# Spreading the experts' weights: two accumulated 128-column products per token, or one of 256 columns with its halves added on GpSimd

## The chip, the cores and the metric

One core of a Trainium2 chip runs the whole program. The metric is the device time of one execution in microseconds; smaller is better. TensorE multiplies, VectorE (DVE in the profile), ScalarE (ACT) and GpSimd (POOL) work on tiles in SBUF, and all DMAs are issued from SyncE's queue (SP).

## The reference, cut to what matters

Two transformer blocks run one after the other on 256 tokens of 1024 features. The second has two layers; each ends in a product-key mixture over 16384 experts, of which a token takes 16 in each of 8 heads. In the first layer 256 tokens of context take part as well.

```python
def peer_block(hb, w_q, sub_keys, u_tab, v_tab):
    ...
    top_s, pos = lax.top_k(cand_s, PEER_TOPK)
    expert = jnp.take_along_axis(cand_i, pos, axis=-1)      # i1 * 128 + i2
    g = jax.nn.softmax(top_s, axis=-1)
    u = u_tab[expert]
    act = jax.nn.gelu(jnp.einsum('nhkd,nd->nhk', u, hb).astype(jnp.float32))
    w = (g * act).astype(hb.dtype)
    return jnp.einsum('nhk,nhkd->nd', w, v_tab[expert])
```

## The kernel before

The kernel gathers no experts. It computes the hidden value of every expert for every token, multiplies it by a weight that is zero for all but the chosen ones, and sums over all experts. For that each token needs its 128 weights `g` spread over a matrix of 128 first keys by 128 second keys.

Arithmetic near float32 is had by cutting each operand in two float32r parts (`split`, lines 198 and 199: a cast on ACT, a subtraction on DVE) and taking three products (`mac`, lines 232 to 234).

The change touches `spread`. For a block of 128 tokens it takes four tokens per turn of a generator: 32 turns for a block, four blocks in the first layer and two in the second, 192 turns in all. One turn does this:

- DVE builds `E` (line 1053, four instructions of 512 float16 values): a one-hot of the first key, a one-hot of the second key, and the second one multiplied by each of two float16 parts of the weight. The four tokens lie side by side, innermost, so that the columns of one token are 4 values (8 bytes) apart.
- TensorE makes, for each token, two products with the same stationary operand: first key's one-hot by each part of the weighted second key's one-hot. Both are of 128 columns, and the second is added to the first in PSUM (line 1057). Eight matmuls, eight weight loads.
- ACT takes the PSUM bank of four tokens to the tile `st`, where a token's values lie 64 bytes apart (line 1058). After four turns SP sends `st` to the memory `Gd` (line 1060).

`pG` is a bank of the PSUM ring `C`, which has four; `E` lies in the ring `wb` (three slots), `st` in `k8` (seven), and the ring `k2` (six) holds the outputs of line 1100 and small tiles of `choose`.

`ahead` runs this beside the main work: it goes through the 128 tiles of experts, and after each tile (`hidden`: a load, the two parts, 24 products of 256 columns per 256 tokens, a gelu on ACT) lets the generators of `choose` and `spread` take as many turns as the plan (`P0`, `P1`) says. So a stretch of `hidden` products alternates with one or two turns of `spread` on TensorE. The hidden values go to the memory `kept`. After `ahead`, `experts` loads the weights (`b<-G`) and the hidden values (`k<-kept`) again and sums.

The order of the instructions on each engine is that of a scheduler which runs when the program is built; each engine then works through its own list in order.

Of the kernel before, what the change touches and what calls it, by code (L numbers as in the profile page):

```python
# [18 lines left out]
P = 128  # L19
# [7 lines left out]
# columns of the first layer's modulation: on the tensor engine; before the experts  # L27
EARLY = 16
MID = 40
# the context's hidden values taken early: tiles up to here beside the first block, and beside the second's start  # L30
FILL = (27, 39)
# the last tiles of experts are summed bank by bank
TAIL = 4
# steps of the work beside: at the points of the mixers, of the feed-forwards (norm, pieces), of the second block's start
# [3 lines left out]
# when the choices, then the spreadings, of the blocks of tokens start, and at what pace  # L38
P0 = ((5, 0.8), (38, 0.95), (72, 1.15), (124, 1.1), (38, 0.9), (83, 0.8), (121, 0.9), (169, 0.95))
P1 = ((5, 0.75), (41, 1.0), (45, 0.5), (85, 0.85))  # L40
# choices that begin beside the scores, of the two layers
EAR = (1, 1)
# tiles of experts whose hidden values the second layer takes before the sums
# [3 lines left out]
class Side:  # L47
    """Where a stream of work keeps its tiles: weights, PSUM for products and transposes, slots."""
# [5 lines left out]
class Net:  # L54
# [19 lines left out]
    @staticmethod  # L74
    def done(gen):
        """all the steps of a generator; its result"""
        while True:
            try:
                next(gen)
            except StopIteration as e:  # L80
                return e.value

    def pace(self, side, rate):
        """other work that goes on beside: `rate` steps of it at each point where the main work lets it in"""
        self.side, self.rate, self.due = side, rate, 0.0
# [7 lines left out]
    def beside(self, gen, n=1):  # L93
        """all the steps of a generator, with `n` breaths after each; its result"""
        while True:
            try:
                next(gen)
            except StopIteration as e:
                return e.value
            self.breathe(n)  # L100

# [42 lines left out]
    def rsqrt(self, ss, n, m, sfx):  # L144
        """(ss / n + eps) ** -0.5 of the columns ss[:m rows]"""
# [8 lines left out]
    def norm_T(self, sd, xt, scale, bias=None, dst=None, between=None):  # L154
        """rms-normalised rows of xt [128, 2, 1024], transposed to [128, 8, 256], times scale plus bias
        (columns [128, 8], a value per feature), in two parts where the side's products want them"""
# [39 lines left out]
    def split(self, hi, lo, src):  # L196
        """src as the sum of two float32r parts"""
        self.nc.scalar.copy(hi, src)  # L198
        self.nc.vector.tensor_sub(lo, src, hi.bitcast(F32))  # L199

    def cut_in_two(self, shape, raw):
        """the two parts of a block of weights, in the ring of slots of the phase"""
# [10 lines left out]
    def weights(self, sd, src, n=512, order=None):  # L213
        """src [128, k, n], row block by row block: two blocks are loaded at a time and cut in two parts"""
# [11 lines left out]
    def mac(self, out, a, b, first, last):  # L226
        """out += a.T @ b, operands in two parts each"""
# [11 lines left out]
    def tok_steps(self, sd, src, hT, order=(0, 2, 4, 6), also=None, apart=False):  # L239
        """hT.T @ src for both blocks of tokens, and for both of `also`: banks [128 tokens, 512];  # L240
        apart: one block after the other, with all the weights at hand"""
# [18 lines left out]
    @staticmethod  # L260
    def cut(f, a, b):
        """the columns a to b of both parts"""
        return tuple(None if t is None else t[:, a:b] for t in f)

# [1 line left out]
    def mixer(self, l, x):  # L266
# [5 lines left out]
        # queries, keys and values of the attention heads, tokens on the partitions  # L272
# [20 lines left out]
        # columns: kc kc | vc vc | ks kw | vs vw | gates | i | f  # L293
# [17 lines left out]
        # windows of 32 tokens, 16 apart, the odd tokens of a window on the upper partitions  # L311
# [11 lines left out]
        # norms and rotation of the attention heads  # L323
# [25 lines left out]
        # gates of the matrix memory  # L349
# [22 lines left out]
        # q and k of the matrix memory: a feature per partition, convolved along the tokens  # L372
# [17 lines left out]
        # the rest of the matrix memory's inputs  # L390
# [14 lines left out]
        # transposes: pairs of heads, the second of a pair on the upper partitions  # L405
# [26 lines left out]
        # compressed keys and values  # L432
# [67 lines left out]
        # attention: groups of four heads (moba, selected, window), of which a unit takes the even or the odd ones  # L500
# [69 lines left out]
        # matrix memory, all tokens at once  # L570
# [155 lines left out]
    def ada_early(self):  # L726
        """the first columns of the first layer's modulation of both streams, a value per feature and partition:
        [128, 2 streams, 6 * 8]; work comes in steps"""
# [17 lines left out]
    def ada_rest(self, i0, i1):  # L746
        """the rest of the first layer's modulation, then the second's: columns i0 to i1 of the two in a row"""
# [23 lines left out]
    def modulation(self, l, part):  # L771
        """the biases, and (1 + scale) * gain in place of the scales; part 0: before attention, part 1: after"""
# [7 lines left out]
    def gate(self, sd, col, n, g=None):  # L780
        """col [128, 8], a value per feature, as a row of 512 features on every partition"""
# [8 lines left out]
    def qkv(self, sd, l, hT, rope, hT2=None):  # L790
        """the heads' queries and keys, normalised and rotated, features by tokens, and the values;
        a chunk of four heads (two of keys, two of values) at a time.
        hT2: of another 256 tokens the keys and values too, not rotated"""
# [3 lines left out]
        if rope:  # L797
            # gain * cos, and the partner's gain * sin
# [20 lines left out]
    def heads(self, sd, n, pks, gain, turn, dst, v):  # L819
        """a chunk's heads of two blocks of tokens from PSUM: normalised, rotated and transposed to dst; or values to v"""  # L820
# [37 lines left out]
    def attention(self, sd, qT, segs, sink=None, window=False):  # L858
        """softmax over the keys of segs [(kT, v)], 256 keys each; the heads' outputs, features by tokens"""
# [79 lines left out]
    def key_scores(self, l, hs, ss):  # L939
        """the scores of the keys, per block of 128 tokens [128 tokens, (head, half), 128 keys], head by head"""  # L940
# [22 lines left out]
    def choose(self, sd, s):  # L963
        """of a block of 128 tokens [128 (head, choice), 4, 128 tokens], float16: the two key numbers and two parts
        of GSCALE times the weight"""
# [29 lines left out]
        # the place in the list gives the ranks of the two keys  # L995
# [46 lines left out]
    def spread(self, r, Gd, nb):  # L1042
        """the weights of a token's experts, a matrix [128 first keys, 128 second keys] per token;
        four tokens per turn of the generator"""
        nc = self.nc
        for q in range(P // NT):
            st = self.t("k8", [P, P, NT])
            for m in range(0, NT, 4):
                n = q * NT + m
                pG = self.p("C", [P, 4, P])  # L1050
# [4 lines left out]
                for j in range(4):  # L1055
                    for i in range(2):
                        nc.tensor.matmul(pG[:, j], E[:, 0, :, j], E[:, 2 + i, :, j], start=i == 0, stop=i == 1)  # L1057
                nc.scalar.activation(st[:, :, m:m + 4], pG.rearrange("p n e -> p e n"), AF.Copy, scale=1 / GSCALE)
# [4 lines left out]
    def routing(self, l, hs, Gd, order, early, plan):  # L1063
        """the scores of the keys, and the rest of the routing as a plan for `ahead`: of the blocks of tokens in order
        [(block, place in Gd)] the choice, then the spreading of the weights;
        the first `early` choices begin beside the scores. plan: when each choice and each spreading starts, and its pace"""
# [17 lines left out]
    def hidden(self, l, e, hs, aside=False):  # L1084
        """gelu(u . h) of the tile e of experts: [128 experts, 256 tokens for each of hs]"""
# [17 lines left out]
    def ahead(self, l, hs, kept, n, plan, done=0):  # L1103
        """the hidden values of the first n tiles, kept in memory while the weights are still to come;
        the first `done` lack the first 256 tokens only.
        plan: [(start, a generator, its turns per 256 tokens of a tile)]"""
# [17 lines left out]
    def experts(self, l, hs, Gd, kept, side):  # L1124
        """sum over all experts of weight * gelu(u . h) * v; hs: functions giving the parts of h for 256 tokens each.
        side: a generator of other work, a step of which goes with every second tile of experts.
        Yields (block of tokens, half of the features, the sums)"""
# [58 lines left out]
    def context(self):  # L1186
        """the context's side of the first layer, which hangs on nothing before it, up to its experts"""
# [21 lines left out]
    def context_end(self):  # L1209
        """the output of the context's attention, and what its experts work on"""  # L1210
# [14 lines left out]
    def fill(self, e0, e1):  # L1225
        """the context's hidden values of the first layer's tiles e0 to e1"""
# [4 lines left out]
    def block2(self, x):  # L1231
# [4 lines left out]
        # the first layer of the stream itself  # L1236
# [28 lines left out]
        # the second layer  # L1265
# [22 lines left out]
def _rows(w):  # L1288
    """[.., 1024, n] -> [.., 128, 8, n]"""
# [4 lines left out]
def _tiles(w, c=512):  # L1294
    """[.., 1024, n * c] -> [.., n, 128, 8, c]"""
# [7 lines left out]
def _cols(v):  # L1303
    """[.., 1024] -> [.., 128, 8]"""
# [4 lines left out]
def layout(i):  # L1309
# [20 lines left out]
    # second block  # L1330
# [17 lines left out]
    # constants  # L1348
# [58 lines left out]
```

## Time and profile before

| | |
|---|---|
| time, median of 3 runs | 3616.06 us |
| lowest and highest run | 3615.57 and 3619.06 us |
| span of the profiled execution | 3617.9 us |
| TensorE busy | 98% of the span |
| VectorE, ScalarE, GpSimd busy | 66%, 42%, 1% |
| turns of `spread` | 192, between 1287 and 3225 us |

The profiled execution shows a span of 3617.9 us, 1.8 us above the median of the runs and inside their range. Records of TensorE overlap, since matmuls are pipelined: a busy share of 98% is time in which some matmul was on its way, and the pace is read from the spacing of the starts or from counts in a stretch.

### The profile page before, as it was taken

The numbers are of one execution on the slowest core, as the hardware profiler recorded it, in microseconds if no ns is written. First come the engines' busy times: TensorE is split into PE (matmuls) and PEld (weight loads), VectorE is DVE, ScalarE is ACT, GpSimd is POOL, SyncE is SP. The second block draws the span as 40 slices with busy tenths as digits, with TensorE's granted clock in tenths as the row PEclk, the third lists the DMA queues.
The fourth block names the chain that finished last, engine by engine and source line by source line (L and its number), as shares of the span: only waits on it lengthen the run. The fifth ranks groups of instructions, "written<-read, shape, count | busy, mean of one in ns | idle before, by whom it ended". The sixth has DMA issues, their size and how long they took to land.

```text
span 3617.9 us, 58159 instructions
## 1 busy us (share of the span) xinstructions
PE 3548.2 (98%) x22400; PEld 3116.1 (86%) x22400; DVE 2372.8 (66%) x5225; ACT 1528.0 (42%) x2557; POOL 51.9 (1%) x72
## 2 busy tenths in 40 slices
PE   8999989999999999999999999999999999999999
PEld 6677776899899999999998888888878999998777
DVE  6666776655754778767647655554476778767666
ACT  5543455544643433333333322222254545545443
POOL 1000010000000000000000000000000000000000
PEclk9999999999999999999999999999999999999999
DMA  6556644566522754445579877776223777779986
GB/s 222 165 181 200 202 154 131 188 202 201 161 94 83 228 181 164 170 171 177 178 239 290 265 246 243 235 225 188 76 77 113 213 232 233 247 268 297 293 256 192
DMA packets 329383, 712.76 MB, mean 197 GB/s; under 512 B 28305, under 2 KB 170257, under 8 KB 322705
## 3 DMA queue, kind: packets, MB, share of 16 engines
q1 hardware_dynamic: 329104, 709.05, 61.4%
q8 instruction: 175, 2.87, 0.3%
q14 instruction: 104, 0.84, 0.1%
HBM read 606.44 MB, written 102.50 MB: 196 GB/s over the span
## 4 chain that ended last, share of the span: by engine, by line
PE 82%; DMA 8%; DVE 6%; issue 1%; ACT 1%; SPq 0%; POOL 0%; DVEq 0%; POOLq 0%; ACTq 0%
PE psA L232 12%; PE psA L233 12%; PE psA L234 12%; PE psC L233 9%; PE psC L234 9%; PE psC L232 9%; PE psC L1057 5%; DMA wb<-in_v 3%; DMA k<-kept 3%; PE psB L233 3%; PE psB L232 3%; PE psB L234 3%; DVE k L199 2%; PE psB L230 1%; DVE ws L199 1%
## 5 line engine op out<-in xcount | busy, mean ns | idle before, releaser
L198 ACT CAST ws<-w 128x1024 fp32r<-128x1024 f32 (+1 forms) x528 | 548.3, 1038 | 1032.0 <-PE psA L233 738.4
L199 DVE TENSOR_TENSOR ws<-w,ws 128x1024 fp32r<-128x1024 f32 (+1 forms) x528 | 636.7, 1207 | 411.5 <-ACT ws L198 405.9
L232 PE MATMUL psA<-b,ws 128*128 128x256 f32 x2760 | 784.7, 284 | 0.0
L234 PE MATMUL psA<-b,ws 128*128 128x256 f32 x2760 | 773.9, 280 | 0.9 <-DVE ws L199 0.3
L233 PE MATMUL psA<-b,ws 128*128 128x256 f32 x2760 | 773.2, 280 | 0.0
L232 PEld LDWEIGHTS psA<-b,ws 128*128 128x128 f32 x2760 | 521.8, 189 | 0.6 <-ACT k L1100 0.2
L234 PEld LDWEIGHTS psA<-b,ws 128*128 128x128 f32 x2760 | 519.3, 188 | 2.6 <-DVE ws L199 2.5
L233 PEld LDWEIGHTS psA<-b,ws 128*128 128x128 f32 x2760 | 520.3, 189 | 0.0
L234 PE MATMUL psC<-k,k 128*128 128x512 f32 x1056 | 417.8, 396 | 8.6 <-DVE k L199 8.1
L232 PE MATMUL psC<-k,k 128*128 128x512 f32 x1056 | 416.0, 394 | 3.7 <-ACT k L198 3.7
L233 PE MATMUL psC<-k,k 128*128 128x512 f32 x1056 | 415.7, 394 | 0.0
L198 ACT CAST k<-wb 128x1024 fp32r<-128x1024 f32 x256 | 268.7, 1050 | 239.1 <-DMA wb<-in_v 238.9
L199 DVE TENSOR_TENSOR k<-wb,k 128x1024 fp32r<-128x1024 f32 x256 | 312.8, 1222 | 56.7 <-ACT k L198 56.4
L198 ACT CAST k<-k 128x256 fp32r<-128x256 f32 (+1 forms) x272 | 137.0, 506 | 445.1 <-PE psA L234 417.2
L1147 DVE TENSOR_TENSOR k<-k,b 128x256 f32<-128x256 f32 x384 | 150.3, 422 | 216.6 <-DMA k<-kept 215.4
L234 PEld LDWEIGHTS psC<-k,k 128*128 128x128 f32 x1056 | 198.3, 188 | 66.6 <-DVE k L199 22.1
L1053 DVE TENSOR_TENSOR wb<-iota,R 128x512 f16<-128x512 f16 x384 | 151.0, 421 | 148.3 <-PE psC L1057 147.6
L233 PE MATMUL psC<-ws,k 128*128 128x512 f32 (+1 forms) x608 | 240.5, 396 | 6.2 <-DVE ws L199 5.1
L232 PEld LDWEIGHTS psC<-k,k 128*128 128x128 f32 x1056 | 198.5, 188 | 48.6 <-ACT k L198 5.1
L232 PE MATMUL psC<-ws,k 128*128 128x512 f32 (+1 forms) x608 | 239.4, 397 | 0.7 <-ACT ws L198 0.3
L234 PE MATMUL psC<-ws,k 128*128 128x512 f32 (+1 forms) x608 | 238.0, 392 | 0.0
L233 PEld LDWEIGHTS psC<-k,k 128*128 128x128 f32 x1056 | 198.6, 188 | 44.3
(399 smaller groups left out, 6359.8 us busy)
## 6 DMA issues: line engine op xcount, KB each, us to landing
w<-in_u SPq DMA_DIRECT2D x256, 512.0 KB, 4.1
wb<-in_v SPq DMA_DIRECT2D x256, 512.0 KB, 4.4
w<-in_w_ff SPq DMA_DIRECT2D x128, 512.0 KB, 4.1
G<-k SPq DMA_DIRECT2D x48, 1024.0 KB, 4.7
b<-G SPq DMA_DIRECT2D x48, 1024.0 KB, 8.3
wb<-in_ada_w SPq DMA_DIRECT2D x80, 512.0 KB, 4.6
k<-kept SPq DMA_DIRECT2D x128, 256.0 KB, 3.9
w<-in_wA SPq DMA_DIRECT2D x48, 512.0 KB, 4.6
```

What stands on the lines that cost most here:

```text
L198: self.nc.scalar.copy(hi, src)
L199: self.nc.vector.tensor_sub(lo, src, hi.bitcast(F32))
L230: self.nc.tensor.matmul(out, ah, bh, start=first, stop=last)
L232: self.nc.tensor.matmul(out, ah, bh, start=first, stop=False)
L233: self.nc.tensor.matmul(out, ah, bl, start=False, stop=False)
L234: self.nc.tensor.matmul(out, al, bh, start=False, stop=last)
L1053: nc.vector.tensor_tensor(E[:, i], self.iota4 if i < 2 else E[:, 1], r[:, i, None, n:n + 4].to_broadcast([P, P, 4]), op=ALU.is_equal if i ...
L1057: nc.tensor.matmul(pG[:, j], E[:, 0, :, j], E[:, 2 + i, :, j], start=i == 0, stop=i == 1)
L1147: nc.vector.tensor_mul(g3, g3, Gs[i][:, :, j])
```

## The change

Each token's two products become one of 256 columns: the two parts of the weighted one-hot, side by side, are streamed against the stationary one-hot, once. Nothing is accumulated in PSUM any more; a token fills 256 columns, and four tokens fill two banks. ACT then takes the first halves of two tokens to `st` and the second halves to a new tile `lo` (from the ring `k2`), in four instructions of 256 values, and GpSimd adds `lo` to `st` in place. The other lines of the diff remove comments.

```diff
             for m in range(0, NT, 4):
                 n = q * NT + m
-                pG = self.p("C", [P, 4, P])
+                pG = [self.p("C", [P, 2, 2, P]) for _ in range(2)]
                 E = self.t("wb", [P, 4, P, 4], F16)
...
                 for j in range(4):
-                    for i in range(2):
-                        nc.tensor.matmul(pG[:, j], E[:, 0, :, j], E[:, 2 + i, :, j], start=i == 0, stop=i == 1)
-                nc.scalar.activation(st[:, :, m:m + 4], pG.rearrange("p n e -> p e n"), AF.Copy, scale=1 / GSCALE)
+                    nc.tensor.matmul(pG[j // 2][:, j % 2], E[:, 0, :, j], E[:, 2:4, :, j], start=True, stop=True)
+                lo = self.t("k2", [P, 4, P])
+                for j in range(0, 4, 2):
+                    nc.scalar.activation(st[:, :, m + j:m + j + 2].rearrange("p e n -> p n e"), pG[j // 2][:, :, 0], AF.Copy, scale=1 / GSCALE)
+                    nc.scalar.activation(lo[:, j:j + 2], pG[j // 2][:, :, 1], AF.Copy, scale=1 / GSCALE)
+                sm = st[:, :, m:m + 4].rearrange("p e n -> p n e")
+                nc.gpsimd.tensor_add(sm, sm, lo)
                 if m == NT - 4:
                     nc.sync.dma_start(Gd[:, nb + q], st)
```

## Rows read from the trace of the kernel before

**Rows 1.** The page: busy time of the engines, and the chain by engine.

```profile
PE 3548.2 (98%) x22400; PEld 3116.1 (86%) x22400; DVE 2372.8 (66%) x5225; ACT 1528.0 (42%) x2557; POOL 51.9 (1%) x72
...
PE 82%; DMA 8%; DVE 6%; issue 1%; ACT 1%; SPq 0%; POOL 0%; DVEq 0%; POOLq 0%; ACTq 0%
```

**Rows 2.** Three spread stretches and eight together; busy us (instructions) per engine.

```profile
1400.00:1500.00 100.00, 100.00 (x853) 99.33 (x852) 87.98 (x336) 34.29 (x51) 0.00 (x0) 1.00 0.50 172
...
1600.00:1700.00 100.00, 100.00 (x852) 99.14 (x851) 80.31 (x289) 37.81 (x56) 0.00 (x0) 1.00 0.49 173
...
3075.00:3175.00 100.00, 100.00 (x849) 98.69 (x847) 74.05 (x152) 50.13 (x83) 0.00 (x0) 1.00 0.71 241
...
sum 825.00, PE 825.00 PEld 817.94 DVE 607.77 ACT 330.55 POOL 0.00; mean PE 103.12 PEld 102.24 DVE 75.97 ACT 41.32 POOL 0.00
```

**Rows 3.** The same three stretches, line 1057 alone: matmuls, then weight loads.

```profile
1400.00:1500.00 100.00, 16.93 (x130) 13.83 (x131) 1.00 0.50 172
...
1600.00:1700.00 100.00, 25.96 (x200) 21.62 (x200) 1.00 0.49 173
...
3075.00:3175.00 100.00, 34.24 (x261) 27.48 (x258) 1.00 0.71 241
```

**Rows 4.** Views of lines 1057 and 1058: nanoseconds min/median/max of one.

```profile
L1057 PEld LDWEIGHTS <-wb x1536: 112/117/139, 1287.5 to 3224.3; 128*128 128x128 f16 x192
L1057 PE MATMUL psC<-wb x1536: 280/297/303, 1287.5 to 3224.5; 128*128 128x128 f16 x192
...
L1058 ACT ACTIVATE k<-psC x192: 581/592/622, 1289.0 to 3225.0; 128x512 f32<-128x512 f32 x192
```

**Rows 5.** Timeline of TensorE: one turn, then two turns in a row.

```profile
1354.47 1.11 PE L1057 MATMUL psC<-wb 128*128 128x128 f16 x8
...
1361.06 2.06 PE L1057 MATMUL psC<-wb 128*128 128x128 f16 x16
```

**Rows 6.** Timeline, products of 512 columns: a first and the fourteenth, evenly spaced.

```profile
2200.03 0.39 PE L233 MATMUL psC<-k,k 128*128 128x512 f32 x1
...
2202.97 0.39 PE L234 MATMUL psA<-k,k 128*128 128x512 f32 x1
```

**Rows 7.** Timeline inside a turn: one weight load, and the matmuls from it on.

```profile
1354.82 0.12 PEld L1057 LDWEIGHTS <-wb 128*128 128x128 f16 x1
...
1354.94 0.54 PE L1057 MATMUL psC<-wb 128*128 128x128 f16 x3
```

**Rows 8.** Line 478: 15 columns per load of 128 weights; one length, then timeline.

```profile
L478 PE MATMUL psC<-kcc,k x32: 258/258/279, 161.1 to 619.8; 64*128 64x15 f32 x32
...
161.24 0.30 PEld L478 LDWEIGHTS psC<-kcc,k 64*128 64x128 f32 x2
...
161.26 0.48 PE L478 MATMUL psC<-kcc,k 64*128 64x15 f32 x3
```

**Rows 9.** Timeline of ACT: a gelu of 256 values from PSUM.

```profile
3152.90 0.38 ACT L1100 ACTIVATE k<-psA 128x256 f32<-128x256 f32 x1
```

**Rows 10.** POOL's own work, a DVE instruction beside it, DVE's 512 float32 values.

```profile
7.37 0.55 POOL L151 TENSOR_TENSOR rsrf<-rsvf,neghalf 128x1 f32<-128x1 f32 x1 [6.92 <-DVE rsvf L150]
...
57.13 6.77 POOL L151 TENSOR_TENSOR rsrf<-rsvf,neghalf 128x16 f32<-128x16 f32 x2 [47.53 <-DVE rsvf L150]
...
61.06 1.23 DVE L333 TENSOR_TENSOR k<-k,rsrf 128x1024 f32<-128x1024 f32 x1 [2.81 <-POOL rsrf L151]
...
L841 DVE TENSOR_TENSOR k<-psC,k x12: 415/684/689, 948.1 to 2684.5; 128x512 f32<-128x512 f32 x8, 128x256 f32<-128x256 f32 x4
```

**Rows 11.** The eight stretches again: DVE's line 1053, then its line 199.

```profile
sum 825.00, DVE 274.19; mean DVE 34.27
...
sum 825.00, DVE 186.88; mean DVE 23.36
```

**Rows 12.** The chain that ended last, and SP's queue, after the last turn.

```profile
3225.57 5.82 DMA G<-k
...
3231.41 0.62 SPq L1140 DMA_DIRECT2D b<-G  x1
3232.13 2.68 SPq L1110 DMA_DIRECT2D kept<-k  x2
```

## The prediction

> **What bounds the kernel now.** I read the page first: TensorE is busy 98% of the span and 82% of the chain that ended last [rows 1]. Then I cut the time in which turns of `spread` run, 1300 to 1850 and 2950 to 3225 us, into eight stretches [rows 2]. The reader is to see three things there. Every stretch holds about 850 matmuls per 100 us, one each 0.117 us, with the clock granted in full. That count is the same whether 130, 200 or 261 of them are line 1057's [rows 3], so a product of 128 columns of `spread` costs as much as one of 256 columns of `hidden`. And DVE is the next engine: 88.0, 80.3 and 74.1 us of 100 in the three fullest stretches, against 34 to 50 for ACT. TensorE sets the pace; whatever makes DVE late by more than its idle time takes over.
>
> The price of a turn comes from the timeline: eight matmuls take 1.11 us and sixteen 2.06 us, their last one's pipeline included [rows 5], so eight more cost 0.95 us, 0.119 each. With the lower 0.118 a turn is 8 x 0.118 = 0.944 us, and 192 turns are 181 us of TensorE.
>
> **The matmuls and weight loads.** Four matmuls of 256 columns and four loads replace eight and eight. The trace has no float16 product of 256 strided columns, so its price has two ends. If loading 128 weights is what takes 0.118 us, the columns are free up to the length of the load, and the new product costs what `hidden`'s 256 columns do, 0.117: a turn falls to 0.468 us and 192 turns give back 0.476 x 192 = 91 us. If the columns themselves take it, 256 cost twice as much, less one start: 512 columns of `hidden`'s kind come every 2.94 / 13 = 0.226 us [rows 6], so 256 at 0.117 hold a fixed 2 x 0.117 - 0.226 = 0.008. Then the new product costs 0.228 to 0.236 us, and 192 turns give back 192 x (0.944 - 0.912) = 6 us down to nothing.
>
> To choose, I looked for a row in which weights do set the pace. Line 478 loads 128 weights for only 15 columns: loads and matmuls come 0.11 us apart, the matmul starts 0.02 us after its load starts, and it ends (0.258 long) at 161.52, when its load, some 0.19 long, has been over since 161.43 [rows 8]. So there a matmul ends 0.09 us after its weights are in. In a turn of `spread` the load runs from 1354.82 to 1354.94, its matmul starts at that end [rows 7] and takes 0.297 us [rows 4]: it ends 0.30 us after its weights are in. That is 0.21 more. The 113 additional columns would account for 0.05 at the pace of rows 6, (0.226 - 0.117) / 256 = 0.43 ns each. The rest is a wait for something other than weights, and what lies in front is the matmul before. So the columns set the pace: 0.118 for 128, which are read 8 bytes apart, is twice the pace of columns side by side. I take the middle of that end, -3 us, and keep -91 us as a rival.
>
> The Trainium skill speaks for the other end. Advanced Engine Details and Errata (SBUF Cachelines) has lines of 16 bytes and full speed from two hits on a line, which 8-byte steps give; by it the columns would not be slow, and the sum would hold -91 instead of -3. No row here shows a strided column at full pace.
>
> **ACT.** One eviction of 592 ns [rows 4] becomes four of 256 values, 0.38 us each by the nearest row, a gelu of that size [rows 9]: +0.93 us per turn at most, 179 us in all. It hides in ACT's idle time: the fullest stretch for it, 3075 to 3175, has 261 / 8 = 32.6 turns, so 50.1 + 30.3 = 80 of 100 us. If that cover went, all 179 us would count. Two banks of `C` per turn leave the ring two turns deep where it was four; between turns lie 24 or 48 `hidden` products, 2.8 or 5.6 us, in which ACT empties both, so I price it at nothing.
>
> **GpSimd's add.** It is new, 512 float32 values, and POOL does nothing in these stretches [rows 2]. Its price from below: DVE needs 0.68 us for as many float32 values. From above: POOL's power function takes 0.55 us for one value per partition and 3.39 for sixteen, 0.19 us each, which would be 97 us; that is a power and no add, so the row nearest is DVE's. I take DVE's 0.68 plus POOL's 0.55 for one value as a start: 1.23 us [rows 10]. At one add per 3.1 us or more (100 / 32.6) POOL keeps up; from 3.1 us on it would set the pace.
>
> What matters is whether DVE runs beside it. The turn's `E` and the subtraction at line 199 read two tensors from SBUF and fill (274.2 + 186.9) / 825 = 56% of the time [rows 11]. The one close row: line 333 on DVE, with two such inputs, starts at 61.06, inside POOL's second power (which runs to 63.9), and takes 1.23 us as always [rows 10]. So there DVE lost nothing; but that POOL instruction reads 16 values, not 1024. The loss per turn lies between nothing and the whole 1.23. DVE's idle time per turn is 12.0 / 16.3 = 0.74, 19.7 / 25 = 0.79 and 25.9 / 32.6 = 0.80 us in the three fullest stretches, and 217 / 192 = 1.13 on average [rows 2, 3]. I take 0.65 x 1.23 = 0.80, a share somewhat over 56% since `choose` has such instructions too. Beyond the idle time it costs 0.06 x 16.3 + 0.01 x 25 = 1.3 us. POOL's own wait for DVE costs nothing unless `k2` runs out: `lo` holds one of six slots for some 3 us a turn.
>
> The skill states a rule against the change here: SBUF — State Buffer (Who interferes with whom) says that a DVE instruction with two SBUF inputs and a reading GpSimd instruction block each other, the second waiting until the first is done. The row at 61.06 does not show it. GPSIMD Engine Reference (Performance versus the Vector engine) gives 4497 ns for an add of 2048 values, an estimated 1.1 us for 512, and its pitfalls add half for reads over 8 bytes apart: 1.7 us. By both, the 1.3 us above would be about 100.
>
> **What is moved.** `G<-k` is issued from SP after POOL instead of ACT, 48 times, some 0.93 + 1.23 = 2.2 us later. Behind it in SP's queue are weight loads a tile or more ahead, which hides all but the last. After that one SP waits at 3231.41 with `b<-G`, and the last stores of `kept` stand behind it and go at 3232.13; this is on the chain [rows 12]. So +2.2 us once. In the first layer the last turn is followed by more tiles of `hidden` before the sums.
>
> **Sum.** 3617.9 - 3 + 1.3 + 2.2 = 3618.4 us of span; the span stands 1.8 us above the median of the runs (3616.06), so about 3617 us.
>
> **Rivals and chances.** Runs spread over 0.1%; I call less than 0.2% (7.2 us) no change.
>
> A, the forecast (0.36): columns set the pace, DVE's loss fits its idle time. 3617, with its own range 3606 to 3627. Within it 0.06 faster, 0.26 the same, 0.04 slower.
>
> B, slower (0.34): the add locks DVE out. It decides from 0.75 us lost per turn on. With all of 1.23: 0.49 x 16.3 + 0.44 x 25 + 0.43 x 32.6 = 33 us, 3650; with an add of 1.6 us, (1.6 - 1.13) x 192 = 90 us, 3707. For it: DVE at 74 to 88%, over half of it two-input. Against: the row at 61.06.
>
> C, faster (0.22): weights set the pace. -91 us; but then DVE's idle time per turn shrinks by 0.476, and a loss of 0.80 costs 0.54 x 16.3 + 0.49 x 25 + 0.48 x 32.6 = 37 us in these stretches. So 3527 (nothing lost) to 3565. For it: weight loads stand end to end, 0.117 us each [rows 4, 7]. Against: rows 8.
>
> D (0.08): C's gain and B's lock together, 0.97 x 16.3 + 0.92 x 25 + 0.91 x 32.6 = 68 us and more given back: 3594 to 3625; 0.04 faster, 0.03 the same, 0.01 slower.
>
> Together faster 0.32, the same 0.29, slower 0.39. The range runs from 3540 to 3680: it leaves out C's far end (0.08) and B's (0.11).
>
> **What would show it.** The start-to-start time of line 1057's new matmuls: near 0.23 us for A and B, 0.12 for C. Line 1053's and 199's mean lengths and DVE's busy share in these stretches: grown in B, as is the wait of line 1057 for DVE. POOL's add: over 3 us would make it the bound, and I would be wrong by a case I gave no chance. ACT under 85% in every stretch.

## The result and the profile after

The changed kernel takes 3668.39 us (median of 4 runs, 3664.70 to 3670.96), the kernel before on the same chip 3615.82 us: a ratio of 1.0143, 95% interval 1.0131 to 1.0156. It is 52.6 us slower. That lies inside the range of the prediction, 3540 to 3680 us, and is rival B, not the forecast of 3617 us.

The lines of the change keep their order in the new file: line 1056 is the product, 1059 and 1060 are ACT's evictions of first and second halves, 1062 is GpSimd's add. `hidden`'s gelu is line 1104.

The page of the changed kernel, against [rows 1]: busy time of the engines and the chain by engine.

```profile
PE 3562.8 (97%) x21632; PEld 3055.9 (83%) x21632; DVE 2592.6 (71%) x5225; ACT 1705.4 (47%) x3133; POOL 429.3 (12%) x264
...
PE 67%; DVE 20%; DMA 7%; issue 3%; ACT 1%; POOL 0%; SPq 0%; DVEq 0%; POOLq 0%; ACTq 0%
```

DVE has as many instructions as before, 5225, and is busy 219.8 us longer; its share of the chain rises from 6% to 20% and TensorE's falls from 82% to 67%. 219.8 us over 192 turns are 1.14 us a turn.

The views of single lines, nanoseconds min/median/max of one.

```profile
L1056 PEld LDWEIGHTS <-wb x768: 111/117/138, 1285.6 to 3277.0; 128*128 128x128 f16 x192
L1056 PE MATMUL psC<-wb x768: 386/409/416, 1285.6 to 3277.2; 128*128 128x256 f16 x192
...
L1059 ACT ACTIVATE k<-psC x384: 590/624/716, 1287.1 to 3278.6; 128x256 f32<-128x256 f32 x192
...
L1060 ACT ACTIVATE k<-psC x384: 375/439/493, 1287.5 to 3279.0; 128x256 f32<-128x256 f32 x192
...
L1062 POOL TENSOR_TENSOR k<-k,k x192: 1555/1780/6998, 1288.7 to 3279.5; 128x512 f32<-128x512 f32 x192
...
L1053 DVE TENSOR_TENSOR wb<-iota,R x384: 397/416/1842, 1279.3 to 3266.7; 128x512 f16<-128x512 f16 x192
L1053 DVE TENSOR_TENSOR wb<-wb,R x384: 397/417/1865, 1280.5 to 3268.6; 128x512 f16<-128x512 f16 x192
```

GpSimd's add takes 1.56 us at the least. The median of line 1053 is what it was, but its longest take 1.84 and 1.87 us: 0.42 and some 1.4 more, nearly a whole add.

The timeline of the changed kernel shows one such meeting. First two turns of matmuls some microseconds later, for their pace; then GpSimd, then VectorE.

```profile
1329.84 2.01 PE L1056 MATMUL psC<-wb 128*128 128x256 f16 x8
...
1325.47 3.28 POOL L1062 TENSOR_TENSOR k<-k,k 128x512 f32<-128x512 f32 x2 [5.11 <-ACT k L1060]
...
1325.42 0.27 DVE L936 MAX8 k<-k 128x8 f32<-128x128 f32 x1
1325.61 1.72 DVE L1053 TENSOR_TENSOR wb<-wb,R 128x512 f16<-128x512 f16 x1
1327.25 0.08 DVE L937 MATCH_VALUE_LOAD k<-k,k 128x8 f32 x1
1327.32 0.28 DVE L937 FIND_INDEX8 k<-k,k 128x8 uint32<-128x128 f32 x1
1327.53 2.31 DVE L199 TENSOR_TENSOR ws<-w,ws 128x1024 fp32r<-128x1024 f32 x1
```

Two adds run from 1325.47 to 1328.75. Line 1053, begun inside the first, takes 1.72 us instead of 0.42; line 199, begun inside the second, 2.31 instead of 1.22 and ends after it. Lines 936 and 937 run beside the adds at their usual length. The same split holds over 1300 to 1850 us, where `choose` (which picks the experts) and `spread` share VectorE: VectorE's groups, count, then busy us and mean ns; first the changed kernel, then the kernel before.

```profile
L1053 DVE TENSOR_TENSOR wb<-wb,R 128x512 f16<-128x512 f16 x222 | 140.2, 660 | 1.2
L1053 DVE TENSOR_TENSOR wb<-iota,R 128x512 f16<-128x512 f16 x224 | 112.8, 537 | 15.5 <-PE psC L1056 15.0
L199 DVE TENSOR_TENSOR ws<-w,ws 128x1024 fp32r<-128x1024 f32 x74 | 111.2, 1504 | 24.9 <-ACT ws L198 24.9
...
L935 DVE MATCH_REPLACE8 k<-k,k 128x128 f32<-128x128 f32 (+1 forms) x68 | 18.0, 267 | 0.0
L936 DVE MAX8 k<-k 128x8 f32<-128x128 f32 (+1 forms) x68 | 17.8, 272 | 0.0
```

```profile
L1053 DVE TENSOR_TENSOR wb<-iota,R 128x512 f16<-128x512 f16 x238 | 93.9, 420 | 90.1 <-PE psC L1057 89.3
L199 DVE TENSOR_TENSOR ws<-w,ws 128x1024 fp32r<-128x1024 f32 x77 | 93.9, 1220 | 39.7 <-ACT ws L198 35.3 <-DMA w<-in_u 4.3
L1053 DVE TENSOR_TENSOR wb<-wb,R 128x512 f16<-128x512 f16 x239 | 91.9, 420 | 1.5
```

Lines 935 and 936 have means of 272 and 277 ns in the kernel before. The instructions that read two tensors from SBUF grow; the ones that search one tensor do not. A few instructions with one input are held too: a cast (line 983) and an operation with a constant (line 1004), each with a single long one in the changed kernel and none in the kernel before. Nanoseconds min/median/max, the changed kernel and then the kernel before:

```profile
L983 DVE CAST k<-k x6: 279/282/1684, 1172.0 to 3016.2; 128x256 f16<-128x256 uint32 x6
L1004 DVE TENSOR_SCALAR k<-k x12: 211/218/1607, 1222.8 to 3072.8; 128x128 uint32<-128x128 uint32 x12
...
L983 DVE CAST k<-k x6: 284/288/292, 1173.9 to 2985.9; 128x256 f16<-128x256 uint32 x6
L1004 DVE TENSOR_SCALAR k<-k x12: 218/221/235, 1224.7 to 3036.9; 128x128 uint32<-128x128 uint32 x12
```

The lock works the other way as well, and the longest adds are of this kind. Here one begins while VectorE goes through its instructions without a pause:

```profile
3137.94 4.90 POOL L1062 TENSOR_TENSOR k<-k,k 128x512 f32<-128x512 f32 x1 [3.58 <-ACT k L1060]
...
3138.16 0.75 DVE L1053 TENSOR_TENSOR wb<-iota,R 128x512 f16<-128x512 f16 x2
3138.83 1.21 DVE L199 TENSOR_TENSOR ws<-w,ws 128x1024 fp32r<-128x1024 f32 x1
3139.96 0.75 DVE L1053 TENSOR_TENSOR wb<-wb,R 128x512 f16<-128x512 f16 x2
3140.63 0.75 DVE L1053 TENSOR_TENSOR wb<-iota,R 128x512 f16<-128x512 f16 x2
```

VectorE's instructions keep their usual length, and the add takes 4.90 us, 1.46 of them after VectorE's row has ended at 3141.38.

What this costs TensorE stands in the waits of its weight loads, in us, times, longest: first 1300 to 1850, then 2950 to 3280 us. The kernel before, from 1300 to 1850 and from 2950 to 3225 us, has none.

```profile
PEld L1056 <- DVE wb L1053: 17.5, 13, 4.2
PEld psA L234 <- DVE ws L199: 5.7, 6, 2.0
PEld psB L1033 <- DVE k L1023: 1.6, 1, 1.6
PEld L1056 <- issue: 1.6, 1, 1.6
PEld L1056 <- PE psA L234: 0.9, 1, 0.9
PEld L1056 <- PE psC L1056: 0.5, 1, 0.5
...
PEld psA L234 <- DVE ws L199: 20.9, 26, 2.0
PEld L1056 <- DVE wb L1053: 1.7, 5, 0.8
PEld L1056 <- PE psA L234: 0.8, 1, 0.8
```

The lines sum to 51.2 us, 47.4 of them for VectorE and none for ACT. The spans of the two profiled executions differ by 48.5 us, the medians by 52.6.

One more thing changes. In the kernel before, the granted clock of TensorE is 1.00 in all eight stretches with turns. In the changed kernel it is below that in five of them. The stretch from 1500 to 1600 us, then the longest wait in it, then the time around its end; the last three numbers of a stretch are the granted clock, the share of the DMA engines and GB/s:

```profile
1500.00:1600.00 100.00, 92.53 (x685) 83.02 (x683) 86.40 (x132) 52.19 (x116) 44.16 (x22) 0.97 0.44 158
...
1519.96 1.09 PE L1056 MATMUL psC<-wb 128*128 128x256 f16 x4 [3.68 <-DVE wb L1053]
...
1518.00:1524.00 6.00, 4.04 (x19) 3.76 (x20) 5.97 (x10) 1.56 (x4) 3.02 (x2) 0.50 0.47 131
```

TensorE stands still for 3.68 us for line 1053; the granted clock falls in that wait to 0.50, which is 1.2 GHz and not 2.4, and the products of `hidden` behind it start 0.21 us apart instead of 0.117. The shares of clock that are lost in the five stretches add up to some 10 us. That is an estimate, and an upper bound of what the clock adds, since TensorE waits for VectorE in part of that time.

### The profile page after: what moved, and what is told of

The parts are those of the page before. It is cut to its first block, busy times and chain, and to the rows that moved or that the text cites. A ratio compares the mean times of both kernels' runs of the same rounds, so it can differ in the third digit from the quotient of the medians.

```text
span 3666.4 us, 57647 instructions
## 1 busy us (share of the span) xinstructions
PE 3562.8 (97%) x21632; PEld 3055.9 (83%) x21632; DVE 2592.6 (71%) x5225; ACT 1705.4 (47%) x3133; POOL 429.3 (12%) x264
## 4 chain that ended last, share of the span: by engine, by line
PE 67%; DVE 20%; DMA 7%; issue 3%; ACT 1%; POOL 0%; SPq 0%; DVEq 0%; POOLq 0%; ACTq 0%
PE psC L233 9%; PE psC L234 9%; PE psC L232 9%; PE psA L234 8%; PE psA L232 8%; PE psA L233 8%; DVE wb L1053 7%; DVE ws L199 4%; DMA wb<-in_v 3%; PE psB L233 3%; PE psB L232 3%; PE psB L234 3%; DMA k<-kept 2%; DVE k L199 2%; PE psC L1056 1%
## 5 line engine op out<-in xcount | busy, mean ns | idle before, releaser
L199 DVE TENSOR_TENSOR ws<-w,ws 128x1024 fp32r<-128x1024 f32 (+1 forms) x528 | 668.6, 1267 | 380.0 <-ACT ws L198 379.0
L232 PE MATMUL psA<-b,ws 128*128 128x256 f32 x2760 | 802.8, 291 | 1.4 <-ACT k L787 1.4
L234 PE MATMUL psA<-b,ws 128*128 128x256 f32 x2760 | 782.2, 283 | 20.7 <-DVE ws L199 19.8
L233 PE MATMUL psA<-b,ws 128*128 128x256 f32 x2760 | 777.6, 282 | 0.0
L1062 POOL TENSOR_TENSOR k<-k,k 128x512 f32<-128x512 f32 x192 | 377.3, 1987 | 970.4 <-ACT k L1060 823.9
L1053 DVE TENSOR_TENSOR wb<-wb,R 128x512 f16<-128x512 f16 x384 | 257.9, 701 | 1.9
L234 PEld LDWEIGHTS psC<-k,k 128*128 128x128 f32 x1056 | 198.0, 188 | 59.5 <-DVE k L199 15.1
L233 PE MATMUL psC<-ws,k 128*128 128x512 f32 (+1 forms) x608 | 240.4, 395 | 4.3 <-DVE ws L199 4.2
L1059 ACT ACTIVATE k<-psC 128x256 f32<-128x256 f32 x384 | 239.2, 626 | 4.1 <-PE psC L1056 4.1
L232 PE MATMUL psC<-ws,k 128*128 128x512 f32 (+1 forms) x608 | 239.2, 397 | 0.8 <-ACT k L183 0.2
L232 PEld LDWEIGHTS psC<-k,k 128*128 128x128 f32 x1056 | 198.2, 188 | 48.6 <-ACT k L198 4.2
```

Of the source, the lines that this page charges most:

```text
L232: self.nc.tensor.matmul(out, ah, bh, start=first, stop=False)
L233: self.nc.tensor.matmul(out, ah, bl, start=False, stop=False)
L234: self.nc.tensor.matmul(out, al, bh, start=False, stop=last)
L1053: nc.vector.tensor_tensor(E[:, i], self.iota4 if i < 2 else E[:, 1], r[:, i, None, n:n + 4].to_broadcast([P, P, 4]), op=ALU.is_equal if i ...
L1059: nc.scalar.activation(st[:, :, m + j:m + j + 2].rearrange("p e n -> p n e"), pG[j // 2][:, :, 0], AF.Copy, scale=1 / GSCALE)
L1062: nc.gpsimd.tensor_add(sm, sm, lo)
```

## The experiments

Two theories stood against each other. The lock theory: GpSimd's add shuts out VectorE's instructions with two SBUF inputs, VectorE falls behind, TensorE waits. The eviction theory: ACT's four evictions and a ring `C` that is two turns deep hold TensorE up. On the columns two more: a column read 8 bytes from the next costs twice the time (columns), or loading 128 weights is what takes 0.118 us (weights). All kernels were timed against the kernel before on the same chip; "+" and "-" are differences from it.

**The change without the add.**

```diff
-                nc.gpsimd.tensor_add(sm, sm, lo)
```

> The change without GpSimd's add: one product of 256 columns per token, both halves evicted by ACT in four instructions, the second halves left in `lo` and never added (so the weights lack their second part). Lock theory (GpSimd's add blocks VectorE's instructions that read two tensors from SBUF): the loss is gone, 3608 to 3624 us, and line 1053 on DVE back at 0.42 us on average where the changed kernel has 0.63. Eviction theory (four evictions take ACT about 2.0 us a turn instead of 0.59, and the ring `C` is two turns deep instead of four): still 3650 to 3670 us. Column theory (a column read 8 bytes from the next costs 0.9 ns): the products stay 0.23 us apart, so there is no gain below 3605 us; by the weight theory they would be 0.12 us apart and the time about 3525 us.

Measured: 3613.58 us against 3617.68, ratio 0.9989 (0.9980 to 0.9999), so -4.1 us. From the page of this kernel:

```profile
PE 3542.9 (98%) x21632; PEld 3047.1 (84%) x21632; DVE 2375.7 (66%) x5225; ACT 1706.6 (47%) x3133; POOL 51.9 (1%) x72
```

With all four evictions and two banks per turn in place the loss is gone, and DVE is back at 2375.7 us. The granted clock is 1.00 in all eight stretches again. The eviction theory falls. The weight theory falls too: no 91 us appear, and the -3 us of the prediction's column step lie inside the interval (-7.2 to -0.4).

**The add alone.**

```diff
                 nc.scalar.activation(st[:, :, m:m + 4], pG.rearrange("p n e -> p e n"), AF.Copy, scale=1 / GSCALE)
+                sm, lo = st[:, :, m:m + 4].rearrange("p e n -> p n e"), self.t("k2", [P, 4, P])
+                nc.gpsimd.tensor_add(lo, sm, sm)
```

> The kernel before with its two accumulated products and one eviction, and after the eviction a GpSimd add of 512 values of `st` to themselves into a tile of the ring `k2` that nobody reads: the add alone. Lock theory: 1.1 us of VectorE lost per turn as in the changed kernel, 3650 to 3675 us, the longest of line 1053 about 1.8 us on DVE. Eviction theory: the add is off the path, 3612 to 3620 us.

Measured: 3625.40 us, ratio 1.0027 (1.0017 to 1.0036), +7.7 us. Lines of this kernel:

```profile
L1053 DVE TENSOR_TENSOR wb<-wb,R x384: 395/416/1343, 1281.6 to 3223.7; 128x512 f16<-128x512 f16 x192
...
L1060 POOL TENSOR_TENSOR k<-k x192: 1073/1282/4513, 1289.0 to 3232.8; 128x512 f32<-128x512 f32 x192
```

The lock is there, and the loss is smaller than expected, because this add is shorter: 1.07 us at the least and not 1.56. DVE is busy 2506.7 us, 0.70 a turn more. So both theories missed the time: the add is not off the path, and 0.70 us a turn is nearly all idle time of VectorE.

**A copy in place of the add** (one tensor read and not two): `nc.gpsimd.tensor_copy(lo, sm)`.

> The kernel before, and after each eviction a GpSimd copy of the 512 values just written in `st` to a tile of `k2` that nobody reads: GpSimd reads one tensor, not two. If any reading instruction of GpSimd shuts out VectorE's instructions with two SBUF inputs, some of line 1053 last as long as the copy besides their 0.42 us (longest 0.9 us or more) and VectorE's busy time grows by some 0.3 to 0.6 us per turn. If only two reading streams of GpSimd against two of VectorE do, the longest of line 1053 stays at 0.43 us. Either way less is lost than VectorE has idle: 3612 to 3622 us.

Measured: 3628.32 us, ratio 1.0028 (1.0019 to 1.0038), +10.6 us, a little over the range. The copy takes 1.06 us at the least, line 1053 up to 1.34, DVE grows by 0.70 us a turn. A GpSimd instruction with one input does the same; adding a tensor to itself is no longer than copying it.

**A power in place of the add**: as long as the add, but it reads two inputs of 8 values and writes 8.

```diff
+                lo = self.t("k2", [P, 16])
+                nc.gpsimd.tensor_tensor(lo[:, :8], self.iota[:, 16:24], self.neghalf[:, :8], op=ALU.pow)
```

> The kernel before, and in each turn a GpSimd power of eight constants per partition into a tile that nobody reads: an instruction as long as the changed kernel's add (1.65 us for eight values) that reads 8 values and not 1024. If GpSimd shuts VectorE out while it runs: line 1053 stretched to 2 us at most, 1.1 us lost per turn, 3650 to 3670 us. If it does so only while it reads tensors: line 1053 at most 0.45 us long, 3612 to 3620 us; then the row at 61.06 could not tell anything of an add.

Measured: 3620.99 us, ratio 1.0005 (0.9995 to 1.0015): no difference clear of noise, and 1 us over the second range. Lines of this kernel:

```profile
L1053 DVE TENSOR_TENSOR wb<-iota,R x384: 406/422/470, 1281.9 to 3216.3; 128x512 f16<-128x512 f16 x192
...
L1060 POOL TENSOR_TENSOR k<-c_iota,neghalf x192: 1629/1802/4807, 1281.5 to 3217.5; 128x8 f32<-128x8 f32 x192
```

GpSimd is busy 444.5 us, more than in the changed kernel, and line 1053 never takes over 0.47 us, though 448 of its 768 instructions of these two kinds begin while a power runs. It is not GpSimd's running that locks VectorE out, but its streaming of tensors. Whether the reading or the writing of SBUF does it is not shown: every GpSimd instruction here that locked did both.

**The sum on VectorE.** No `lo`, no GpSimd; instead of the second eviction:

```diff
+                    nc.vector.scalar_tensor_tensor(sm, pG[j // 2][:, :, 1], 1 / GSCALE, sm, ALU.mult, ALU.add)
```

> The change with the halves summed by VectorE and not by GpSimd: ACT evicts the first halves (two instructions of 256 values), VectorE multiplies the second halves, read from PSUM, by the scale and adds them to `st` (two instructions). Lock theory: GpSimd is silent, nothing is stretched; VectorE has 2 x 0.42 us = 0.83 us more to do per turn, a little more than its idle time in the fullest stretches and less than the 1.14 us per turn that it loses now: 3616 to 3645 us. Eviction theory: ACT has 1.2 us a turn instead of 2.0, but VectorE's two reads of PSUM come behind it, so the banks come free no sooner: 3650 to 3670 us.

Measured: 3640.61 us, ratio 1.0059 (1.0042 to 1.0076), +22.9 us, where the lock theory put it, but by another price: the two instructions take 0.62 us each and not 0.42. DVE's busy time, in which records that overlap count once, grows by 193.2 us, 1.01 a turn. Nothing is locked here: line 1053 takes 0.48 us at most. Less than half of the loss is there without any lock, by VectorE's time alone.

**The sum to another place**: `tensor_add(lo, sm, lo)`, one operand changed.

> The changed kernel with one operand changed: GpSimd writes the sum to `lo`, side by side, and not back to `st` with steps of 64 bytes (so `st` keeps the first halves alone). The evictions, the ring of two turns and both reads are as in the changed kernel. Lock theory with the loss set by the add's length: 1.3 us per add and 0.7 us lost per turn as in the kernel before with the add alone, 3615 to 3630 us. If the remaining 45 us between that kernel and the changed one come from the evictions beside the add: 3645 to 3670 us.

Measured: 3665.18 us, ratio 1.0133 (1.0116 to 1.0150), +47.5 us. That is the second range, and my account of the add's length falls: the add takes 1.53 us at the least, and GpSimd's busy time is 418.7 us against 429.3, so writing back in steps of 64 bytes costs almost nothing. VectorE is locked as long as before (DVE 2588.1 us, 1.12 a turn). Since the add stayed long, the run does not tell a long add from evictions beside an add; against the evictions speaks that the waits of TensorE's loads in the changed kernel name VectorE and never ACT. The kernel with the add alone had a short add; it read one tensor twice, and here two different ones are read, which may be the reason and was not tried by itself.

**The same work walked key by key**: `lo` as `[P, P, 4]`, evictions and add in groups of 8 and 16 bytes.

> The changed kernel with the same four evictions and the same add, walked key by key and not token by token: `lo` holds four tokens innermost as `st` does, so the add reads and writes groups of 16 bytes and the evictions write groups of 8 bytes, instead of single values 64 bytes apart. If the steps of 64 bytes are what makes the add 1.7 us long, it falls to about 1.1 to 1.3 us, the loss on VectorE to 0.6 to 0.8 us per turn, and the time to 3612 to 3630 us; ACT's first halves fall from 0.63 us to about 0.4. If the add's length does not hang on the steps: 3655 to 3675 us.

Measured: 3634.69 us, ratio 1.0048 (1.0031 to 1.0065), +17.0 us, a little over the range. Lines of this kernel:

```profile
L1062 POOL TENSOR_TENSOR k<-k,k x192: 1266/1466/6251, 1291.5 to 3250.4; 128x512 f32<-128x512 f32 x192
...
L1059 ACT ACTIVATE k<-psC x384: 370/410/483, 1290.2 to 3249.6; 128x256 f32<-128x256 f32 x192
```

The add is 0.29 us shorter, the longest of line 1053 falls from 1.87 to 1.56 us, DVE grows by 0.85 us a turn, and the loss of time to a third. ACT's first halves fall from 0.62 to 0.41 us.

**Columns 4 bytes apart, in the kernel before.** `E` holds its tokens in two pairs, and line 1053 writes them in that order:

```diff
-                E = self.t("wb", [P, 4, P, 4], F16)
+                E = self.t("wb", [P, 4, 2, P, 2], F16)
...
-                        nc.tensor.matmul(pG[:, j], E[:, 0, :, j], E[:, 2 + i, :, j], start=i == 0, stop=i == 1)
+                        nc.tensor.matmul(pG[:, j], E[:, 0, j // 2, :, j % 2], E[:, 2 + i, j // 2, :, j % 2], start=i == 0, stop=i == 1)
```

> The kernel before with one thing changed: `E` holds its four tokens in two pairs, so that the columns of one token lie 4 bytes apart and not 8; two accumulated products of 128 columns, no GpSimd. Column theory: a column at 4 bytes costs 0.43 to 0.45 ns instead of 0.9, a product of 128 falls from 0.118 us to 0.06 us or to what a load of 128 weights takes (0.11 us by line 478's spacing): 192 x 8 x (0.118 - 0.11 to 0.06) = 12 to 90 us less, 3526 to 3604 us. Weight theory (loading 128 weights is what takes 0.118 us): nothing changes, 3612 to 3620 us. If VectorE takes longer for line 1053 with the new order of values (over 0.6 us each instead of 0.42), the kernel is slower, over 3640 us.

Measured: 3543.61 us against 3617.68, ratio 0.9787 (0.9771 to 0.9803), -74.1 us. This is the whole computation, and it beats both kernels. Two turns on its TensorE, against 2.06 us in [rows 5], and its line of loads:

```profile
1300.83 1.09 PE L1058 MATMUL psC<-wb 128*128 128x128 f16 x16
...
L1058 PEld LDWEIGHTS <-wb x1536: 95/97/103, 1287.5 to 3148.5; 128*128 128x128 f16 x192
L1058 PE MATMUL psC<-wb x1536: 217/219/237, 1287.5 to 3148.6; 128*128 128x128 f16 x192
```

Less the last one's 0.22 us, fifteen starts take 0.87 us: 0.058 each instead of 0.118, with as many loads of as many weights. The weights lie 4 bytes apart here too, and their load is shown with 97 ns instead of 117. That the loads did not set the pace is shown by the changed kernel: it has half as many, with the wide step, and its 256 columns still take 0.229 us. So the columns set the pace. DVE stays at 2372.6 us.

**Both together, with and without the add.** One product of 256 columns, 4 bytes apart.

> The changed kernel with `E` in two pairs of tokens, so that the columns of one token lie 4 bytes apart: four products of 256 columns at 0.12 us instead of 0.23, GpSimd's add kept. TensorE has 0.45 us less per turn, 86 us in all. VectorE sets the pace (lock theory): it loses 1.1 us per turn as before, TensorE's time given back is time in which VectorE would have to work, so most of the 86 us do not show: 3620 to 3665 us, and line 1053 waited for much longer than the 33 us of the changed kernel. TensorE sets the pace and the add only delays single turns: 3575 to 3595 us.

> One product of 256 columns per token, columns 4 bytes apart, both halves evicted by ACT, and no GpSimd: the kernel in pairs with one product and the add, less the add (so the weights lack their second part). Lock theory: TensorE's 86 us come through at once, 3530 to 3550 us, as in the kernel in pairs with two products, and the add alone costs some 115 us there, twice what it costs with slow columns. Eviction theory (ACT's four evictions or the ring of two turns hold TensorE up once it is faster): 3580 to 3655 us.

Measured: with the add 3656.79 us, ratio 1.0111 (1.0094 to 1.0128); without it 3531.59 us, ratio 0.9765 (0.9748 to 0.9781). TensorE's work is the same in both. 1600 to 1700 us, with the add and then without it: busy us (instructions) of PE, PEld, DVE, ACT, POOL.

```profile
1600.00:1700.00 100.00, 88.24 (x708) 84.51 (x707) 98.22 (x303) 55.92 (x121) 40.34 (x24) 0.95 0.46 151
```

```profile
1600.00:1700.00 100.00, 100.00 (x844) 98.45 (x844) 71.35 (x212) 54.41 (x109) 0.00 (x0) 1.00 0.52 179
```

Without the add TensorE is full and 87 us come through; with it VectorE is full, TensorE is not, and of the same gain 13 us are left against the changed kernel (+39.1 instead of +52.6). The add costs 57 us when TensorE is slow (52.6 + 4.1) and 126 when it is fast (39.1 + 87.1). TensorE's loads wait 101 us for VectorE in the stretches with turns where it is fast, 47.4 in the changed kernel. The granted clock in these lines is 0.95 with the add and 1.00 without, so a part of the loss is the clock, which falls where TensorE waits.

**In a row** the kernels show where VectorE's idle time ends. The difference from before, by what DVE's busy time grew per turn (over 2372.8 us, by 192):

| kernel | DVE busy, us | per turn, us | time, us |
|---|---|---|---|
| add alone | 2506.7 | 0.70 | +7.7 |
| copy alone | 2506.4 | 0.70 | +10.6 |
| walked key by key | 2535.2 | 0.85 | +17.0 |
| sum on VectorE | 2566.0 | 1.01 | +22.9 |
| sum to another place | 2588.1 | 1.12 | +47.5 |
| the change | 2592.6 | 1.14 | +52.6 |

From 0.70 to 1.14 us a turn, 86 us of VectorE, the time grows by 45 us; most of that comes from 1.01 us on. The rows differ in more than VectorE's time: the sum on VectorE locks nothing, and the kernel walked key by key has other evictions. The clock differs too: it is granted in full in all eight stretches of the first two rows, below that in one stretch each of the next two, in four for the sum to another place and in five for the change.

## Why the forecast was wrong, though the range held

The range of 3540 to 3680 us held because it was drawn for rivals on both sides. The forecast inside it, no change with the lock hidden in VectorE's idle time, did not. Rival B, at 0.34, named the mechanism; its two figures, 33 and 90 us, lie on both sides of the 52.6. No row stood behind the add of 1.6 us in the second, which came out near (1.56 us at the least), and its formula counts the whole add as lost.

**The columns: right.** I took 0.228 to 0.236 us for a strided product of 256. Eight in a row take 2.01 us; less the last one's 0.41, seven starts take 1.60, 0.229 each. The change without the add gave -4.1 us against the -3 of the sum, and the columns in pairs show the reason. Rival C had the size of TensorE's gain near (91 us; 87 came through with columns 4 bytes apart, without the add) and its condition wrong. Rival D put that gain and the lock together at 3594 to 3625 us; the kernel that has both takes 3656.8, so D too made the lock too cheap. The Trainium skill's rule in Advanced Engine Details and Errata (SBUF Cachelines), full speed from two hits on a line of 16 bytes, does not hold here for the columns that TensorE reads: at 8 bytes they come at half the pace that they have at 4 (0.118 against 0.058 us per 128).

**ACT: right in its sum, and hidden.** I took at most 4 x 0.38 us, +179 us in all; ACT's busy time grew by 177.4 (1705.4 less 1528.0). That is partly luck. The row of a gelu writes side by side; the first halves go to `st` 64 bytes apart and take 0.62 us, the second halves 0.44, together some 2.1 us a turn instead of 1.52. But the four overlap, and overlapping time counts once in busy time. It costs nothing, as the change without the add shows, nor does the shorter ring `C`.

**GpSimd's add: too cheap.** I took 1.23 us; it takes 1.56 at the least and 1.78 in the median. The estimate of 1.7 us that the prediction set beside it was nearer. Single ones last up to 7.0 us; the one of 4.90 us shown above begins while VectorE's instructions keep GpSimd out. Walked key by key the least is 1.27.

**VectorE's loss: the step that failed.** The prediction took "0.65 x 1.23 = 0.80" us a turn and let idle time hide all but 1.3 us of it. The share was too small and the size too: 1.14 us a turn is 0.73 of the least add, and TensorE waits 47.4 us for VectorE. I had thinned it with the row at 61.06, where "DVE lost nothing" inside a power on GpSimd [rows 10]. The power experiment shows that this row could not tell: GpSimd's power of 8 values runs for 1.63 us and more and locks nothing. I had noted that it reads 16 values, not 1024, and still let it weigh against the lock. The Trainium skill's rule in SBUF — State Buffer (Who interferes with whom), as I quoted it, agrees with the traces: two-input instructions of VectorE waited out adds and copies of GpSimd (line 1053 up to 1.87 us), and an add waited out VectorE's (4.90 us). My quotation names two-input instructions alone; here a cast and an operation with a constant waited too (1.68 and 1.61 us).

**The idle time: right in its place, too generous in its use.** Rival B was to decide "from 0.75 us lost per turn on". 0.70 us cost 8 to 11 us, 1.14 cost 53. But by B's own formula 1.14 us would cost 0.40 x 16.3 + 0.35 x 25 + 0.34 x 32.6 = 26 us, half of what was measured. An idle share averaged over 100 us is not all to be had: in the changed kernel, 1300 to 1850 us, VectorE still waits 24.9 us for ACT at line 199 and 15.0 us for TensorE at line 1053, while TensorE waits for VectorE elsewhere. Nor has the formula a term for the clock: where TensorE waited, the granted clock fell, which adds at most some 10 us. That these waits and the clock are why the formula falls short is read from the trace and was not tried.

**The store of `G`: not seen.** The chain after the last turn runs over line 199 and the weight loads, so the 2.2 us of the sum are not on it.

So the sum went wrong by one term: +1.3 us for the lock, where 47 us of waits for VectorE stand, and the clock that fell in them.

What stays open: why the kernel in pairs with two products gains 74 us and the one with one product and no add 87, when their TensorE takes the same 0.058 us per 128 columns (the profiled executions differ by 19 us, and only 6 of them lie in the stretches with turns, 1287.5 to 1814.6 and 2899.7 to 3148.6 us against 1284.0 to 1806.1 and 2886.7 to 3134.8); why an add of two different tensors takes GpSimd 0.46 us longer than one of a tensor to itself; how much of the 52.6 us is the clock; and why some instructions with one input were held and the searches were not.

## What to carry to other kernels

The sum that TensorE made in PSUM took no time of VectorE or GpSimd. Before such a sum is moved to GpSimd, list what VectorE reads from SBUF at that time: here each add took 0.7 of its length from VectorE, and a GpSimd instruction of the same length that reads and writes little told nothing of that. When two products seem bound by their count, look first at how far apart their columns lie: here a layout with 4 bytes between columns was worth 74 us, and joining the products 4, with the sum of the halves left out. An engine's idle time is not all to be had: of VectorE's 1.13 us per turn, 0.70 could be filled for 8 to 11 us in all, and the next 0.44 cost 45 more.

## What the runs showed of the hardware

- TensorE's float16 columns of 128 partitions: 0.118 us per 128 at 8 bytes between columns, 0.058 at 4, with the clock granted in full. A load of 128 weights shows 0.117 us with the wide step and 0.097 with the narrow one, and does not set the pace.
- VectorE's instructions with two SBUF inputs were stretched by up to the length of a GpSimd add or copy less some 0.1 us (0.42 to 1.87 with adds of 1.56 us, 0.42 to 1.34 with copies of 1.06), and by nothing beside a power of 1.63 us. A cast and an operation with a constant, of one input each, were held as well (0.29 to 1.68 and 0.22 to 1.61 us), searches of one tensor never. In turn an add that began in a row of two-input instructions took 4.90 us.
- Writing 256 float32 values 64 bytes apart takes ACT 0.62 us, and VectorE 0.62 us where it adds one input from PSUM to one that lies 64 bytes apart too; ACT takes 0.41 us in groups of 8 bytes.
- TensorE's granted clock was 1.00 in all stretches with turns before the change. After it, it fell to 0.50 in a wait of TensorE of 3.68 us, and products of 256 columns then came 0.21 us apart instead of 0.117.
